# Retention and latent attention block: side work of VectorE moved behind the feature stage, first group's q, k, v copied by ScalarE with its gates ahead of its tiles

## The chip, the cores and the metric

The kernel runs on one core of one Trainium2 chip. The metric is the device time of one execution in microseconds (us). A core has five engines with their own instruction streams: PE (TensorE, matrix products), DVE (VectorE), ACT (ScalarE), POOL (GpSimd) and SP (SyncE, which here only issues DMAs). They wait for each other through semaphores. SBUF is the on-chip memory; PSUM is the memory that PE writes, in eight banks.

## The reference

One encoder block on x, 1024 positions by 1024 features in float32. A modulation that depends on c scales and shifts the normalised x; one combined projection feeds two groups. Group A is retention in 8 heads: rotated q and k, v, a decay per head, chunks of 128 positions in both directions, a normalisation per head, and a SiLU gate. Group B is latent attention in 8 heads. Both are joined by an output projection, and added to x through a modulated gate. The part that matters here, for one direction (shortened):

```python
mask = diff >= 0 if include_diag else diff > 0
decay_intra = jnp.where(mask[None], jnp.exp(lg * jnp.maximum(diff, 0.0)[None]), 0.0)
scores = jnp.einsum('bhnik,bhnjk->bhnij', qc, kc) * decay_intra[None, :, None]
intra = jnp.einsum('bhnij,bhnjv->bhniv', scores, vc)
kv_chunk = jnp.einsum('bhnjk,bhnjv->bhnkv', kc * k_decay[None, :, None, :, None], vc)
def step(state, kv):
    return state * chunk_decay + kv, state
cross = jnp.einsum('bhnik,bhnkv->bhniv', qc * q_decay[None, :, None, :, None], states)
```

## The kernel before, in words

Each float32 product is three matmuls of reduced operands: `mm3` (L64) adds hi by hi (L65), hi by lo (L66) and lo by hi (L67). The hi half of an operand is a cast by ScalarE, the lo half is the subtraction raw minus hi. For weights that is `split` (L75): the cast is L80 on ACT, the subtraction L81, on POOL unless `eng` says otherwise. A weight page of 128x1024 is loaded by `wpage` (L84) into `wr` (two buffers) and then split into `wh` and `wl` (seven buffers each).

*The opening.* For each of 8 tiles of 128 rows, `x_tile` (L148) squares x on ACT (L156) or, for the tiles in `XDVE`, on DVE (L152), raises the mean to the power -0.5 on POOL (L158), scales on DVE (L159), transposes on PE (L163, eight blocks of 128x128), and copies the two PSUM banks out, the first by ACT (L166), the second by DVE (L168). For each of 8 blocks k of 128 features, `modulation(k)` (L174) makes two numbers per feature with two 128x1024 products on DVE (L178) and two small steps (L181, L183), and `features(k, half)` (L186) applies them on ACT (L188), casts to hi on ACT (L189) and subtracts to lo on DVE (L190). `products(k, lo, hi)` (L199) then adds block k to q, k and v of four tiles of the first head group; all eight PSUM banks hold these sums (`acc0`, four of the tag acc, four of sm). That is 192 matmuls of 512 columns. The pages of the first group's weights are split on DVE (L196).

*Side work.* L235 to L260 compute the logarithms of the decays (`lg`, `kfac`), L267 `qfac` by an exponential on ACT, L270 and L271 the operands of the eight masks on DVE, L272 their exponentials on ACT, L274 a scale. L280 to L316 compute the rotary angles in `rtmp` on DVE (reduction in the steps of L291), and `Sr` and `Cr` by a sine on ACT (L313, L316). ACT loads another table when the function changes its set.

*The four head groups.* For each group g the loop over 8 tiles (L344) takes the projected tile (for g = 0 from `acc0`, else from 24 new matmuls), copies v out by ACT (L355), for four banks of group 0 also q and k (`xq`, L360), rotates q and k on DVE (L364, L366) and POOL (L370, L371), prepares kd (L374), transposes on PE (L379), copies qT and kz by ACT (L381, L384), multiplies by the decays (L386), makes scores (L390) and masks them (L392), makes the chunk's k-v product (L397), and folds it into the running state `ST` (L401 to L408). A backward recurrence on DVE ends it (L411). Then come the gate of two heads, 96 matmuls of 512 columns per head (`gate`, L418), whose SiLU by ACT is `sg` (L426), and two `outputs` (L429): products of scores and states (L437, L438), a copy by ACT (L440), statistics (L443), normalisation (L450). `finish` (L453), which transposes (L457), scales by the gate (L459) and stores, waits in a list `pending` until `turn_outputs` (L333) runs it behind a chosen product.

*What sets the order.* The program is written in the order above, but a scheduler moves the instructions of each engine by estimated times, within their dependencies and within the reach of buffers; each engine then runs its own list strictly in that order. `tc.issue_after(x)` says that an instruction is not put ahead of x. The constants at the end of the file (`XDVE`, `KACT`, `PEND` and others) choose these places. A PSUM bank or a buffer is free for its next use when the last reader has ended.

## Time and profile before

| quantity | value |
|---|---|
| median of 3 runs | 1044.26 us (1044.09 to 1044.92) |
| profiled execution, its own time | 1045.73 us |
| span of the profile, first to last instruction | 1043.7 us |
| PE busy | 1011.9 us, 97% of the span |
| DVE, ACT, POOL busy | 562.5, 431.0, 395.2 us |
| mean granted clock of PE | 0.987 |

Busy means that an instruction of the engine was under way. The granted clock is the share of its full clock that PE was given; a value of 1 is 2.4 GHz. An execution's own time is that of its span and what lies around it. In a timeline a row that ends in x16 is a run of 16 like instructions with the time of all; the number in brackets is the idle time before it and what ended it.

### The profile page before, as it was taken

How to read it: one execution, taken by the hardware profiler on the slowest of the kernel's cores; microseconds unless marked ns; L12 is line 12 of the kernel's file. 1: busy time of each engine (PE TensorE's matmuls, PEld its weight loads, DVE VectorE, ACT ScalarE, POOL GpSimd, SP SyncE). 2: the span in 40 equal slices, each digit the busy share in tenths (PEclk: the TensorE clock that was granted, in tenths of full speed). 3: DMA queues.
4: the chain of work that ended last, by engine and by line, in shares of the span. 5: the costliest groups of instructions: out<-in, count | busy, mean ns of one | idle time of the engine just before them, and what ended most of it. 6: DMA issues, size and time to landing. Idle time of an engine off the chain costs nothing.

```text
span 1043.7 us, 15236 instructions
## 1 busy us (share of the span) xinstructions
PE 1011.9 (97%) x5704; PEld 883.0 (85%) x5704; DVE 562.5 (54%) x1287; ACT 431.0 (41%) x873; POOL 395.2 (38%) x359
## 2 busy tenths in 40 slices
PE   5899999999999999999999999999999999989998
PEld 4677888888888888998888889889999999878887
DVE  7995447445444434046302116857777777883342
ACT  6654213312311321224322007577777776762100
POOL 3233315313321522224653213633456544864110
PEclk6999999999999999999999999999999999999999
DMA  9721103101211202323554520100000000004422
GB/s 372 264 66 56 41 1 112 50 1 62 66 36 41 66 27 86 110 93 130 185 175 159 191 94 11 41 1 2 21 21 21 2 21 22 21 21 129 164 101 71
DMA packets 30744, 82.27 MB, mean 79 GB/s; under 512 B 3536, under 2 KB 4560, under 8 KB 30672
## 3 DMA queue, kind: packets, MB, share of 16 engines
q1 hardware_dynamic: 25920, 72.92, 20.8%
q10 hardware_dynamic: 4752, 8.39, 2.2%
q8 instruction: 45, 0.74, 0.3%
q14 instruction: 27, 0.22, 0.1%
HBM read 64.52 MB, written 16.78 MB: 78 GB/s over the span
## 4 chain that ended last, share of the span: by engine, by line
PE 47%; DVE 4%; POOL 1%; ACT 1%; issue 1%; DMA 0%; ACTq 0%; POOLq 0%; DVEq 0%
PE pt L772 5%; PE sp L65 4%; PE sp L66 4%; PE sp L67 4%; PE acc L67 4%; PE acc L66 4%; PE acc L65 4%; PE po L66 3%; PE po L67 3%; PE po L65 3%; PE sm L66 1%; PE sm L65 1%; PE sm L67 1%; PE pt L685 1%; DVE q L659 1%; PE pt L66 1%
## 5 line engine op out<-in xcount | busy, mean ns | idle before, releaser
L81 POOL TENSOR_TENSOR wl<-wr,wh 128x1024 fp32r<-128x1024 f32 (+2 forms) x51 | 115.3, 2268 | 129.8 <-ACT wh L80 111.7
L65 PE MATMUL acc<-wh,hh 128*128 128x512 f32 (+2 forms) x352 | 130.4, 370 | 1.7 <-ACT hh L189 1.7
L66 PE MATMUL acc<-wl,hh 128*128 128x512 f32 (+2 forms) x352 | 130.3, 370 | 0.0
L67 PE MATMUL acc<-wh,hl 128*128 128x512 f32 (+2 forms) x352 | 126.4, 367 | 1.9 <-DVE hl L190 1.9
L758 POOL TENSOR_SCALAR pr<-pr,st 128x1024 f32<-128x1024 f32 x62 | 71.0, 1148 | 101.2 <-DVE st L757 70.0
L65 PE MATMUL acc<-hh,wh 128*128 128x512 f32 x256 | 101.9, 398 | 2.2 <-ACT v L355 2.2
L775 DVE TENSOR_TENSOR pl<-pt,ph 128x512 fp32r<-128x512 f32 x128 | 85.7, 684 | 32.0 <-ACT ph L774 32.0
L66 PE MATMUL acc<-hl,wh 128*128 128x512 f32 x256 | 101.5, 396 | 0.0
L67 PE MATMUL acc<-hh,wl 128*128 128x512 f32 x256 | 101.1, 395 | 0.0
L80 ACT CAST wh<-wr 128x1024 fp32r<-128x1024 f32 (+2 forms) x55 | 53.7, 982 | 106.4 <-PE sm L66 36.6
L774 ACT CAST ph<-pt 128x512 fp32r<-128x512 f32 x128 | 73.3, 590 | 27.1 <-PE pt L772 25.1
L753 DVE TENSOR_REDUCE st<-sp 128x1 f32<-128x1024 f32 x62 | 75.4, 1216 | 8.0 <-PE sp L67 7.9
L66 PE MATMUL po<-pl,vh 128*128 128x256 f32 x256 | 76.0, 297 | 2.3 <-DVE pl L775 2.3
L756 ACT ACTIVATE pr<-sp,st 128x1024 f32<-128x1024 f32 x62 | 69.5, 1122 | 20.7 <-DVE st L754 20.5
L370 POOL TENSOR_TENSOR rb<-t,t 128x128 f32<-128x128 f32 x32 | 16.0, 501 | 161.9 <-PE sm L379 61.2
L65 PEld LDWEIGHTS acc<-wh,hh 128*128 128x128 f32 x352 | 66.9, 190 | 10.6 <-ACT hh L189 2.3
L67 PEld LDWEIGHTS acc<-wh,hl 128*128 128x128 f32 x352 | 66.0, 188 | 10.6 <-DVE hl L190 2.7
L66 PEld LDWEIGHTS acc<-wl,hh 128*128 128x128 f32 x352 | 66.9, 190 | 8.5
L65 PE MATMUL po<-ph,vh 128*128 128x256 f32 x256 | 73.3, 286 | 0.0
L772 PE MATMUL pt<-ident,pr 128*128 128x128 f32 x496 | 69.8, 273 | 2.8 <-DVE st L757 1.2
L67 PE MATMUL po<-ph,vl 128*128 128x256 f32 x256 | 72.4, 283 | 0.0
L772 PEld LDWEIGHTS pt<-ident,pr 128*128 128x128 f32 x496 | 57.6, 140 | 7.3 <-issue 1.4
(361 smaller groups left out, 2449.0 us busy)
## 6 DMA issues: line engine op xcount, KB each, us to landing
x<-w_ada SPq DMA_DIRECT2D x16, 512.0 KB, 6.8
wr<-w_ret SPq DMA_DIRECT2D x16, 512.0 KB, 3.5
wr<-w_rg SPq DMA_DIRECT2D x8, 512.0 KB, 3.5
retD<-ro SPq DMA_DIRECT2D x16, 256.0 KB, 2.0
wr<-w_mg SPq DMA_DIRECT2D x8, 512.0 KB, 3.6
wa<-w_ada SPq DMA_DIRECT2D x8, 512.0 KB, 3.6
wr<-w_out SPq DMA_DIRECT2D x8, 512.0 KB, 4.0
wro<-retD SPq DMA_DIRECT2D x8, 512.0 KB, 3.9
```

The source lines that it names most:

```text
L65: T.matmul(out, lh, rh, start=first, stop=False, **kw)
L66: T.matmul(out, lh, rl, start=False, stop=False, **kw)
L67: return T.matmul(out, ll, rh, start=False, stop=last, **kw)
L80: A.copy(out=hi, in_=raw)
L81: eng.tensor_tensor(out=lo, in0=raw, in1=hi, op=ALU.subtract)
L370: G.tensor_tensor(out=rv[:, :, 0], in0=t1[:, :, 0], in1=t2[:, :, 1], op=ALU.subtract)
L753: V.tensor_reduce(out=st_[:, 0:1], in_=sp, op=ALU.max, axis=AX.X)
L756: A.activation(pr, sp, AF.Exp, bias=st_[:, 1:2], scale=sc_, accum_out=st_[:, 2:3])
L758: G.tensor_scalar(out=pr, in0=pr, scalar1=st_[:, 3:4], scalar2=0.0, op0=ALU.mult, op1=ALU.add)
L772: T.transpose(tp[:, ts_(q)], pr[:, ts_(half * 4 + q)], ident)
L774: A.copy(out=ph[half][:, :, c_], in_=tv)
L775: V.tensor_tensor(out=pl[half][:, :, c_], in0=tv, in1=ph[half][:, :, c_], op=ALU.subtract)
```

## The change

The square of tile 3 goes from DVE to ACT, and for tiles 0 to 3 ACT makes both copies out of PSUM. The two small steps of `modulation` go to ACT. The polynomial for the decays is issued behind a subtraction of feature block 1 (`KDEC`), masks and angles behind that of block 5 (`KACT`). In group 0, ACT copies v and q, k of all eight tiles out of PSUM into SBUF; the gate is computed ahead of the tiles, with its two weight pages split on DVE and not on POOL, issued behind the features of block 6 (`KWG`); the tiles follow the last product of the first head's gate. The weight pages of groups 0 and 1 are issued behind the last features, and both output halves of group 0 are turned in group 1, at tiles 1 and 2.

```diff
@@ -81,10 +81,10 @@
         eng.tensor_tensor(out=lo, in0=raw, in1=hi, op=ALU.subtract)
         return hi.rearrange(*shape[0], **shape[1]), lo.rearrange(*shape[0], **shape[1])
 
-    def wpage(src, n, k, pool=None, tag="wr", bufs=2):
+    def wpage(src, n, k, pool=None, tag="wr", bufs=2, eng=G):
         raw = (pool or p_ring).tile([P, n], F32, name="wr", tag=tag, bufs=bufs)
         SY.dma_start(out=raw, in_=src)
-        return split(raw, (("p (k n) -> p k n",), {"k": k}))
+        return split(raw, (("p (k n) -> p k n",), {"k": k}), eng=eng)
 
     ps1 = ExitStack()
     pp = ps1.enter_context(tc.tile_pool(name="ps1", bufs=1, space=PSUM, reuse_waits="tile"))
@@ -162,7 +162,7 @@
             for q in range(4):
                 T.transpose(ps[:, ts_(q)], x_[:, ts_(4 * z + q)], ident)
             dst, src = xn[:, 4 * z:4 * z + 4, ts_(t)], ps.rearrange("p (a b) -> p a b", a=4)
-            if z == 0:
+            if z == 0 or t < 4:
                 A.copy(out=dst, in_=src)
             else:
                 V.tensor_copy(out=dst, in_=src)
@@ -178,17 +178,16 @@
             V.scalar_tensor_tensor(out=wa, in0=wa, scalar=1.0, in1=sc, op0=ALU.mult, op1=ALU.mult,
                                    accum_out=mp[:, i:i + 1])
         b1 = p_st.tile([P, 2], F32, name="b1", tag="b1", bufs=3)
-        V.scalar_tensor_tensor(out=b1[:, 0:1], in0=mp[:, 0:1], scalar=nw[:, k:k + 1], in1=c1[:, k:k + 1],
-                               op0=ALU.mult, op1=ALU.add)
-        V.tensor_tensor(out=b1[:, 1:2], in0=mp[:, 1:2], in1=bada[:, k:k + 1], op=ALU.add)
+        A.activation(b1[:, 0:1], mp[:, 0:1], AF.Identity, bias=c1[:, k:k + 1], scale=nw[:, k:k + 1])
+        A.activation(b1[:, 1:2], mp[:, 1:2], AF.Identity, bias=bada[:, k:k + 1])
         b1s[k] = b1
 
     def features(k, half):
         sl = slice(half * 512, half * 512 + 512)
         A.activation(xn[:, k, sl], xn[:, k, sl], AF.Identity, bias=b1s[k][:, 1:2], scale=b1s[k][:, 0:1])
         i0 = A.copy(out=hh[k][:, sl], in_=xn[:, k, sl])
-        V.tensor_tensor(out=hl[k][:, sl], in0=xn[:, k, sl], in1=hh[k][:, sl], op=ALU.subtract)
-        return i0
+        i1 = V.tensor_tensor(out=hl[k][:, sl], in0=xn[:, k, sl], in1=hh[k][:, sl], op=ALU.subtract)
+        return i0, i1
 
     w0, acc0 = [], []
 
@@ -227,8 +226,16 @@
             if k or half:
                 i0 = features(k, half)
                 products(k, 4 * half, 4 * half + 4)
+            if k == KDEC:
+                v_first = i0[1]
+            if k == KWG:
+                f_wg = i0[0]
             if k == KACT:
-                x_last = i0
+                x_last, v_last = i0
+
+    f_last = i0[0]
+    late = ExitStack()
+    late.enter_context(tc.issue_after(v_first.ins))
 
 
     lg = ctile("lg", 16)
@@ -259,6 +266,8 @@
     A.activation(kfac[:, :, 1], lg[:, 8:16], AF.Exp, scale=rowc[:, 1:2])
     V.tensor_scalar(out=kfac, in0=kfac, scalar1=0.125, scalar2=None, op0=ALU.mult)
 
+    late.close()
+    late.enter_context(tc.issue_after(v_last.ins))
     qfac = p_rc.tile([P, H, P], F32, name="qfac", tag="qfac")
     mask = p_rc.tile([P, H, P], F32, name="mask", tag="mask")
     after = ExitStack()
@@ -316,6 +325,7 @@
     A.activation(Cr, nn, AF.Sin)
     after.__exit__(None, None, None)
 
+    late.close()
     st.close()
 
 
@@ -336,28 +346,62 @@
             pending.pop(0)()
 
     for g in range(4):
+        after = ExitStack()
+        if g < 2:
+            after.enter_context(tc.issue_after(f_last.ins))
         w = w0 if g == 0 else [wpage(I["w_ret"][g][j], 1024, 2) for j in range(4)]
-        vv = []
+        after.close()
+        vv, xqs = [], []
+
+        wg, sg = [], []
+
+        def gate_begin():
+            sg.append(p_ret.tile([P, 2, S], F32, name="sg", tag="sg"))
+            with tc.issue_after(f_wg.ins):
+                wg.extend(wpage(I["w_rg"][g][j], 1024, 4, eng=V if g == 0 else G) for j in range(2))
+
+        def gate(h):
+            for half in range(2):
+                ps = acc()
+                for k in range(KT):
+                    wh, wl = wg[k // 4]
+                    rh = hh[k][:, half * 512:half * 512 + 512]
+                    rl = hl[k][:, half * 512:half * 512 + 512]
+                    last = mm3(ps, wh[:, k % 4, ts_(h)], wl[:, k % 4, ts_(h)], rh, rl, k == 0, k == KT - 1)
+                A.activation(sg[0][:, h, half * 512:half * 512 + 512], ps, AF.Silu)
+            return last
+
+        if g == 0:
+            for t in range(NT):
+                vv.append(p_ret.tile([P, 2, P], F32, name="v", tag="v", bufs=9))
+                xqs.append(p_ret.tile([P, 2, P], F32, name="xq", tag="sT", bufs=8).rearrange("p a b -> p (a b)"))
+                A.copy(out=xqs[t], in_=acc0[t][:, 0:256])
+                A.copy(out=vv[t].rearrange("p h d -> p (h d)"), in_=acc0[t][:, 256:512])
+            gate_begin()
+            last = gate(0)
+            gate(1)
+            after = ExitStack()
+            after.enter_context(tc.issue_after(last.ins))
         ST = p_ret.tile([P, NT, 2, P], F32, name="ST", tag="ST")
         sT = [None] * NT
         qdT = [None] * NT
         for t in range(NT):
-            if g == 0 and t < NB0:
+            if g == 0:
                 ps = acc0[t]
+                v_ = vv[t]
             else:
                 ps = acc()
                 for k in range(KT):
                     wh, wl = w[k // 2]
                     last = mm3(ps, hh[k][:, ts_(t)], hl[k][:, ts_(t)], wh[:, k % 2], wl[:, k % 2], k == 0, k == KT - 1)
-                if pending and t == PEND:
+                if pending and t in (PEND, PEND + 1):
                     turn_outputs(last)
-            v_ = p_ret.tile([P, 2, P], F32, name="v", tag="v", bufs=9)
-            A.copy(out=v_.rearrange("p h d -> p (h d)"), in_=ps[:, 256:512])
-            vv.append(v_)
+                v_ = p_ret.tile([P, 2, P], F32, name="v", tag="v", bufs=9)
+                A.copy(out=v_.rearrange("p h d -> p (h d)"), in_=ps[:, 256:512])
+                vv.append(v_)
             xq = ps[:, 0:256]
-            if g == 0 and NACC <= t < NB0:
-                xq = p_ret.tile([P, 256], F32, name="xq", tag="o", bufs=5)
-                A.copy(out=xq, in_=ps[:, 0:256])
+            if g == 0:
+                xq = xqs[t]
             xq = xq.rearrange("p (a d) -> p a d", d=32)
             t1 = p_ret.tile([P, 4, 2, 32], F32, name="t1", tag="t1", bufs=2)
             t2 = p_ret.tile([P, 4, 2, 32], F32, name="t2", tag="t2", bufs=2)
@@ -406,25 +450,13 @@
                                                op0=ALU.mult, op1=ALU.add)
             if t > 0:
                 A.copy(out=ST[64:128, t - 1], in_=kvv[64:128])
+        if g == 0:
+            after.close()
         for t in range(NT - 2, 0, -1):
             for h in range(2):
                 V.scalar_tensor_tensor(out=ST[64:128, t - 1, h], in0=ST[64:128, t, h],
                                        scalar=gch[64:128, 2 * g + h:2 * g + h + 1], in1=ST[64:128, t - 1, h],
                                        op0=ALU.mult, op1=ALU.add)
-
-
-        wg = [wpage(I["w_rg"][g][j], 1024, 4) for j in range(2)]
-        sg = p_ret.tile([P, 2, S], F32, name="sg", tag="sg")
-        def gate(h):
-            for half in range(2):
-                ps = acc()
-                for k in range(KT):
-                    wh, wl = wg[k // 4]
-                    rh = hh[k][:, half * 512:half * 512 + 512]
-                    rl = hl[k][:, half * 512:half * 512 + 512]
-                    last = mm3(ps, wh[:, k % 4, ts_(h)], wl[:, k % 4, ts_(h)], rh, rl, k == 0, k == KT - 1)
-                A.activation(sg[:, h, half * 512:half * 512 + 512], ps, AF.Silu)
-            return last
 
         def outputs(half):
             mv = p_ret.tile([P, 4, 2, 2], F32, name="mv", tag="mv", bufs=2)
@@ -457,10 +489,15 @@
                         T.transpose(tp[:, ts_(q)], ob[q][:, h], ident)
                     ro = p_ret.tile([P, 512], F32, name="ro", tag="ro", bufs=2)
                     V.scalar_tensor_tensor(out=ro, in0=tp, scalar=gnw[:, 2 * g + h:2 * g + h + 1],
-                                           in1=sg[:, h, half * 512:half * 512 + 512], op0=ALU.mult, op1=ALU.mult)
+                                           in1=sg[0][:, h, half * 512:half * 512 + 512], op0=ALU.mult, op1=ALU.mult)
                     SY.dma_start(out=retD[2 * g + h, :, half * 512:half * 512 + 512], in_=ro)
             pending.append(finish)
 
+        if g == 0:
+            outputs(0)
+            outputs(1)
+            continue
+        gate_begin()
         gate(0)
         outputs(0)
         last = gate(1)
@@ -921,7 +958,7 @@
 PREP_0 = (2, 4, 5, 6, 6)
 NB0, NACC, XW = 8, 4, 8
 WLX = (6, 7)
-XDVE, KACT = (3, 6), 1
+XDVE, KDEC, KACT, KWG = (6,), 1, 5, 6
 MG0 = 2
 PEND = 1
 EARLY = (2, 6)
```

Three places show how the lists of the engines change. The rows have line, operation, output from input, shape. The first is ScalarE from the last features to the first copies out of PSUM; `Sr`, `Cr` are the rotary tables, `mask` and `mt` the decay masks and their operands. Before:

```order
L272 ACTIVATE mask<-mt 128x128 x2
L189 CAST hh_91<-xn 128x512 x2
L272 ACTIVATE mask<-mt 128x128 x2
L80 CAST wh<-wr 128x1024
L313 ACT_TABLE_LOAD
L313 ACTIVATE Sr<-rtmp 128x256
L316 ACTIVATE Cr<-rtmp 128x256
L80 CAST wh<-wr 128x1024
L355 COPY v<-acc 128x256 x4
L355 COPY v<-sm 128x256
L360 COPY xq<-sm 128x256
```

and now:

```order
L263 ACTIVATE gch<-lgs 128x8
L276 ACTIVATE qfac<-small,lgs 128x128 x8
L325 ACT_TABLE_LOAD
L325 ACTIVATE Cr<-rtmp 128x256
L281 ACT_TABLE_LOAD
L281 ACTIVATE mask<-mt 128x128 x2
L80 CAST wh<-wr 128x1024
L281 ACTIVATE mask<-mt 128x128 x2
L80 CAST wh<-wr 128x1024
L281 ACTIVATE mask<-mt 128x128 x4
L378 COPY xq<-acc 128x256
L379 COPY v<-acc 128x256
```

The factors and masks, which stood between the features, stand behind them, next to the tables, and the copies stand behind all of it.

The second is VectorE around the last feature subtractions (`hl_97` to `hl_99` are the lo halves of blocks 5 to 7). Before:

```order
L190 TENSOR_TENSOR hl_97<-xn,hh_89 128x512
L271 SCALAR_TENSOR_TENSOR mt<-small,lg,m_693 128x128
L190 TENSOR_TENSOR hl_97<-xn,hh_89 128x512
L295 TENSOR_TENSOR rtmp<-rtmp 128x256
L291 SCALAR_TENSOR_TENSOR rtmp<-rtmp 128x256
L270 TENSOR_SCALAR m_699<-small,lg 128x128
L190 TENSOR_TENSOR hl_98<-xn,hh_90 128x512
L291 SCALAR_TENSOR_TENSOR rtmp<-rtmp 128x256
L271 SCALAR_TENSOR_TENSOR mt<-small,lg,m_699 128x128
L190 TENSOR_TENSOR hl_98<-xn,hh_90 128x512
L291 SCALAR_TENSOR_TENSOR rtmp<-rtmp 128x256
L270 TENSOR_SCALAR m_705<-small,lg 128x128
```

and now:

```order
L189 TENSOR_TENSOR hl_97<-xn,hh_89 128x512 x2
L289 CAST posf<-pos 128x8
L189 TENSOR_TENSOR hl_98<-xn,hh_90 128x512 x2
L249 TENSOR_TENSOR lt_627<-lt_626 128x16
L292 TENSOR_TENSOR rtmp<-small,posf 128x256
L189 TENSOR_TENSOR hl_99<-xn,hh_91 128x512
L252 TENSOR_TENSOR lt_628<-lt_628,lt_627 128x16
L296 TENSOR_SCALAR rtmp<-rtmp 128x256
L311 COPY rtmp<-rtmp 128x256
L81 TENSOR_TENSOR wl<-wr,wh 128x1024
L253 TENSOR_SCALAR lt_628<-lt_628 128x16
L297 TENSOR_SCALAR rtmp<-rtmp 128x256
L81 TENSOR_TENSOR wl<-wr,wh 128x1024
```

The mask operands and angle steps that stood between the subtractions have moved behind them, and two page subtractions (L81) have come in ahead of the last.

The third is TensorE at tiles 6 and 7 of group 0 (`qT`, `kz` are operands of the scores, `rb` rotated q and k, `ST` the states, `hh`, `hl`, `wh`, `wl` the operands of a 512-column product). Before:

```order
L65 MATMUL acc<-wh,hh_90 128x512
L66 MATMUL acc<-wl,hh_90 128x512
L67 MATMUL acc<-wh,hl_98 128x512
L390 MATMUL sm<-qT,kz_753 128x128 x2
L397 MATMUL sm<-v,kd 128x128 x2
L437 MATMUL sm<-v,sT 128x128 x2
L65 MATMUL acc<-wh,hh_91 128x512
L66 MATMUL acc<-wl,hh_91 128x512
L67 MATMUL acc<-wh,hl_99 128x512
```

and now:

```order
L434 MATMUL sm<-qT,kz_753 128x128 x2
L441 MATMUL sm<-v,kd 128x128 x2
L423 MATMUL sm<-ident,rb_750 128x128 x3
L65 MATMUL acc<-wh,hh_91 128x512
L66 MATMUL acc<-wl,hh_91 128x512
L67 MATMUL acc<-wh,hl_99 128x512
L434 MATMUL sm<-qT,kz_752 128x128
L441 MATMUL sm<-v,kd 128x128 x2
L434 MATMUL sm<-qT,kz_752 128x128
L423 MATMUL sm<-ident,rb_751 128x128 x3
L434 MATMUL sm<-qT,kz_753 128x128 x2
L441 MATMUL sm<-v,kd 128x128 x2
L469 MATMUL sm<-v,sT 128x128 x4
```

The 512-column products that stood between the steps of the last tiles and the outputs now stand ahead of them and behind them.

## Rows read from the trace of the kernel before

**Rows 1.** The waits of PE: line, waited for, total us, times, longest.

```profile
PE sm L65 <- ACT hh L189: 2.6, 1, 2.6
...
PE acc L65 <- ACT v L355: 2.2, 1, 2.2
...
PE acc L67 <- DVE hl L190: 1.9, 1, 1.9
...
PE sm L67 <- DVE hl L190: 0.9, 1, 0.9
...
PE sm L457 <- DVE o L450: 0.6, 1, 0.6
```

**Rows 2.** Busy us (instructions) by stretch, all engines; PEclk; DMA share; GB/s.

```profile
20.00:30.00 10.00, 8.79 (x39) 7.39 (x40) 10.00 (x22) 4.87 (x8) 3.76 (x2) 0.64 1.03 409
...
80.00:90.00 10.00, 7.91 (x30) 6.44 (x31) 7.21 (x16) 7.50 (x19) 7.46 (x8) 0.83 0.29 93
```

**Rows 3.** Timeline of PE: start, duration, line, operation, idle before.

```profile
33.36 0.50 PE L65 MATMUL sm<-wh,hh 128*128 128x512 f32 x1 [2.60 <-ACT hh L189]
...
79.50 0.39 PE L67 MATMUL sm<-wh,hl 128*128 128x512 f32 x1
82.09 0.77 PE L65 MATMUL acc<-hh,wh 128*128 128x512 f32 x1 [2.20 <-ACT v L355]
82.65 0.63 PE L66 MATMUL acc<-hl,wh 128*128 128x512 f32 x1
```

**Rows 4.** Groups of VectorE by form, 10 to 73 us: count, busy us, mean ns.

```profile
L190 DVE TENSOR_TENSOR hl<-xn,hh 128x512 fp32r<-128x512 f32 x16 | 12.9, 818 | 0.0
...
L270 DVE TENSOR_SCALAR m<-small,lg 128x128 f32<-128x128 f32 x8 | 4.4, 550 | 0.0
L181 DVE SCALAR_TENSOR_TENSOR b<-mp,small,c 128x1 f32<-128x1 f32 x8 | 3.8, 470 | 0.0
...
L271 DVE SCALAR_TENSOR_TENSOR mt<-small,lg,m 128x128 f32<-128x128 f32 x8 | 2.7, 341 | 0.0
L168 DVE COPY xn<-acc 128x512 f32<-128x512 f32 x4 | 2.7, 682 | 0.0
```

**Rows 5.** Timeline of VectorE, late features.

```profile
49.21 3.41 DVE L178 SCALAR_TENSOR_TENSOR x<-x,sc 128x1024 f32<-128x1024 f32 x1
...
72.29 0.68 DVE L190 TENSOR_TENSOR hl<-xn,hh 128x512 fp32r<-128x512 f32 x1
...
77.36 0.88 DVE L291 SCALAR_TENSOR_TENSOR rtmp<-rtmp 128x256 f32<-128x256 f32 x2
```

**Rows 6.** Timeline of POOL at 45 us.

```profile
45.60 5.93 POOL L81 TENSOR_TENSOR wl<-wr,wh 128x1024 fp32r<-128x1024 f32 x2 [18.62 <-ACT wh L80]
```

**Rows 7.** Timeline of ScalarE, 36 to 88 us.

```profile
37.61 1.86 ACT L267 ACTIVATE qfac<-small,lgs 128x128 f32<-128x128 f32 x6
...
78.60 0.42 ACT L313 ACTIVATE Sr<-rtmp 128x256 f32<-128x256 f32 x1 [3.65 <-DVE rtmp L310]
...
79.84 1.04 ACT L80 CAST wh<-wr 128x1024 fp32r<-128x1024 f32 x1
80.79 1.19 ACT L355 COPY v<-acc 128x256 f32<-128x256 f32 x4
...
87.44 0.54 ACT L384 COPY kz<-sm 64x128 f32<-64x128 f32 x2
```

**Rows 8.** Timeline of ScalarE at the start: a table load and the next instruction.

```profile
3.77 1.28 ACT L238 ACT_TABLE_LOAD   x1
5.06 0.22 ACT L238 ACTIVATE lt<-lt 128x16 f32<-128x16 f32 x1
```

**Rows 9.** Timeline of VectorE, groups 0 and 1.

```profile
137.16 3.31 DVE L411 SCALAR_TENSOR_TENSOR ST<-ST,gch 64x128 f32<-64x128 f32 x12 [0.42 <-ACT ST L408]
...
150.96 2.15 DVE L450 TENSOR_SCALAR o<-o,mv,rst 128x128 f32<-128x128 f32 x8 [2.06 <-POOL rst L62]
157.47 1.41 DVE L459 SCALAR_TENSOR_TENSOR ro<-sm,small,sg 128x512 f32<-128x512 f32 x2 [4.36 <-PE sm L457]
```

## The prediction

> **What bounds the kernel now.** I read the waits of PE first, because PE is busy for 97% of the span and a change can win only where PE stands still. [rows 1] have all there is of that between the opening's transposes and the last groups: 2.6 us at the first steady product (it waits for a cast of ScalarE), 1.9 and 0.9 us at products that wait for the low half from VectorE, 2.2 us at the first gate product (it waits for a PSUM bank, which a copy of v frees), and 0.6 us at the outputs of the retention groups. So the most that the opening can give back is these 7.6 us and whatever lets the first product start earlier.
>
> Second, the busy time by stretch of 10 us [rows 2]: VectorE reads 10.00 of 10 (the six stretches from 10 to 70 us read 9.96 to 10.00), so in the features VectorE sets the pace and PE follows. The timeline of PE gives three marks [rows 3]: the steady products start at 33.36, the last one at 79.50, the gate at 82.09. With a spacing of 0.227 us the products end near 79.73. Behind the 2.2 us of standing, the first gate products are 0.43 us apart instead of 0.227, and the mean granted clock of 80 to 90 us is 0.83 [rows 2]: PE runs at 1.2 GHz and not 2.4 for about 3 us after an idle stretch.
>
> Third, what VectorE does there, by kind [rows 4], and single instructions [rows 5]. A modulation product of 1.22 us takes 3.41 us at 49.21, while POOL subtracts two weight pages [rows 6]. The same 2.1 to 2.2 us is in the totals of L270 (4.4 us for eight of 0.28), of L181 (3.8 us for eight of 0.21) and of L190 (12.9 us for sixteen of 0.68). So one page that POOL subtracts can hold VectorE for about 2.2 us; it happened four times in the features, 9 us in all.
>
> **The change, part by part.**
>
> *VectorE's features end earlier.* They take 61.9 us now, from 11.0 to 72.9, where the last L190 ends [rows 5]. What leaves that stretch, by [rows 4]: mask operands 4.4 + 2.7; the small bias L181 3.8, and about 1 for L183; the PSUM copies of the first four tiles 2.7; one square, about 1.2; the angle steps, seven L291 at no more than 0.44 [rows 5], 2.9, with their companions and the polynomial about 2.6; the locks in L178 and L190, 2.2 each. That is 25.7 us busy. Consecutive instructions overlap by some 0.07 us, 3 us over 45 of them, so 22.7 us of time. Two gate pages that VectorE now subtracts itself add 2.3, small steps 1.3. So 43 us of work remain. It can no longer run without a gap, since it will wait for casts and loads; I take 4 us of that (0 to 8). The features end on VectorE at 58 (54 to 62), 15 us earlier.
>
> *PE's features.* The first steady product waits for a chain in which about 3 us of VectorE's work no longer stands (0 to 6): 30.3. With the 2.8 us of waits on L190 gone, the last product ends at 79.73 - 3.06 - 2.96 = 73.7 (the two waits with a few tenths beside them). The 0.2% that a measurement of this kernel can tell from no change is 2.1 us; up to here the change would be worth 6 us.
>
> *The gate can't start there.* Now the side work is late. In the new order of ScalarE, the copies that free the PSUM banks stand behind Sr, kfac, eight qfac, Cr, eight masks and two page casts, and Sr stands behind nearly all angle steps on VectorE. Before, ScalarE did qfac and masks inside the features, and only Sr, Cr and one cast stood ahead of the copies, with Sr waiting 3.65 us for VectorE [rows 7]. From the end of VectorE's features: ten L291 at 0.34 to 0.44, and 25 smaller steps at about 0.1 to 0.3, 6.3 us to Sr's input; two page subtractions of POOL fall there at 2.2 us each, a third perhaps: 10.9 to 13.3. Then on ScalarE [rows 7, 8]: Sr 0.42, table load 1.28, kfac and chunk factors 0.5, qfac 8 x 0.31 = 2.5, load 1.28, Cr 0.42, load 1.28, masks 8 x 0.25 = 2.0, two casts 2.1, two copies 0.7: 12.5. Together 23.4 to 25.8. Two more pages can lock the mask operands, 0 to 4.4 us; I take half, because it hangs on when the pages land. The sum is 26.4 behind 58: the gate starts at 84.4 and not 82.09, **+2.3 us**. Its bounds: not before PE's last product plus a cast, four masks and two copies, 76.4 (-5.7), and not behind 62 + 30 with every lock, less what the loads hide, 89 (+7). I don't go to the ends, because both halves of this chain are priced by rows. PE stands for some 11 us there; the slow 3 us behind it existed before.
>
> The Trainium skill, SBUF — State Buffer, section Who interferes with whom, says that VectorE and GpSimd hold a shared port as a lock for a whole instruction, and that an instruction with two SBUF inputs or a tensor-scalar one in a fast mode is exposed to it. Every mask operand is of these kinds; by that rule alone both pages would lock, and the gate would start 2.2 us later than I take, the total then being 1058.0. [rows 5] agree as to the price, and no run here yet shows whether those pages meet the masks.
>
> The Trainium skill, ScalarE: Activation LUTs, section What ACT_TABLE_LOAD costs, adds a drain of about 1.4 us to every load; with three loads on this path that would be some 4 us more by an estimate from that page. [rows 8] disagree: after a load of 1.28 us the next instruction starts 1.29 us after the load's start.
>
> *New stretches with nothing to fill them.* Before, group 0's tiles ran between gate products and group 1's q, k, v products, and PE lost nothing there beyond 0.6 us. Now the gate's 192 products come first or early and three places hold only tile and output steps. (1) Tiles 6 and 7 with outputs 0: copies of qT and kz 0.9 [rows 7], a copy of the state 0.5, eleven steps of the backward recurrence at 3.31 / 12 = 0.276 [rows 9], 3.0, two rope products 0.75 ahead of the next bank, less 0.8 of PE's own work, 4.35; a smaller wait ahead of it 0.5. (2) The transposes of the first outputs, with a tile: two L459 steps 1.4 [rows 9], copies 0.9, ropes on VectorE 0.75 and on POOL 0.85: 3.9. (3) The second half's transposes behind four normalising steps at 2.15 / 8 = 0.27 [rows 9]: 1.0. Sum 9.75, less the 0.6 that goes: **+9.2 us** (2 if the steps run ahead of PE; 12 at most if PE falls to 1.2 GHz after each).
>
> *At nothing:* the copies of q, k, v out of all banks (16 at 0.27 to 0.30 us apiece on ScalarE [rows 7]): behind the first two PE has 43 us of gate products to cover them. The later loads of group 1's pages: they are due 40 us later. If the gate were short of them it would show as a wait for a cast of L80. POOL loses two subtractions.
>
> *Sum.* 2.3 + 9.2 = +11.5. The profiled execution took 1045.73 us (span 1043.7, 2.0 around it), so 1057.2 on its terms; it was 1.47 above the median of the runs, 1044.26, so 1055.8 against that.
>
> **The rivals.**
> - *Cover holds.* The features end early on VectorE (54 or so), POOL's pages land between its steps and not on them, and the gate starts at 76.4 to 77; tile steps run ahead of PE and lose only 2 us. For it: VectorE has 15 us of new room. Against: ScalarE's 12.5 us remain. Gain 5.7 - 2 to 3, time **1041**, chance 0.16. It decides at a gate start below 78.
> - *Nothing won.* Gate at 78.5 (-3.6), the three stretches 3.6: **1044.3**, chance 0.08.
> - *Only the gate is late.* +2.3 and the stretches lose under 1: **1046.9**, chance 0.17. For it speaks that PE lost 0.6 in such places; against it, that then q, k, v products stood between.
> - *All of it.* Locks on the masks, gate at 89 (+7), the stretches 9.2, and 3 us more at 1.2 GHz: **1063**, chance 0.12.
> - *ScalarE takes over the features*, since it gets the copies, the square and sixteen small steps: then PE's features end at 79 or so, but the gate is set by the side work in any case, and the sum stays. It is part of the forecast.
>
> **How the numbers follow.** Forecast 0.47 at 1055.8, its own range 1051 to 1060. Faster 0.16 is the first rival; same 0.08 the second; slower the rest, 0.76. Range: from 1042.5, which leaves out most of the first rival, to 1063, which leaves out the worst of the last.
>
> **What would show it.** VectorE's last L189 near 58; PE's last feature product near 73.7; a wait of PE of 9 to 12 us at the first gate product, released by a copy on ScalarE; POOL's page subtractions over VectorE's angle steps with 2 us extra each; waits of PE at the outputs and transposes of group 0 of 4 and 4 us where there were none. The forecast is wrong if the gate starts before 78, or if PE's waits from there to group 2 add up to less than 4 us.

## The result, and the profile after

The changed kernel takes **1060.17 us** (median of 5 runs, 1058.96 to 1061.23), the kernel before 1044.92 in the same comparison (5 runs). The ratio is 1.0144, 95% interval 1.0133 to 1.0155: 15.2 us slower. The forecast was 1055.8 with a range of 1042.5 to 1063, so sign and range held, and the loss was some 4 us larger (15.2 for 11.5). The profiled execution took 1060.17 us with a span of 1058.0; against [rows 1], [rows 2] and [rows 3] this is what changed. The page has the engines' busy time, and the group that carries the loss:

```profile
PE 1012.6 (96%) x5704; PEld 883.7 (84%) x5704; DVE 552.9 (52%) x1267; ACT 442.3 (42%) x902; POOL 387.8 (37%) x357
...
L65 PE MATMUL acc<-hh,wh 128*128 128x512 f32 x256 | 102.2, 399 | 14.7 <-ACT v L379 13.8
```

PE does the same work (1012.6 us busy, 1011.9 before) and stands still for longer. The waits of PE (line, waited for, total us, times, longest), where [rows 1] had 2.6 + 2.2 + 1.9 + 0.9 + 0.6:

```profile
PE acc L65 <- ACT v L379: 13.8, 1, 13.8
...
PE sm L65 <- ACT hh L188: 3.1, 1, 3.1
...
PE sm L434 <- ACT kz L428: 2.0, 3, 0.7
...
PE sm L470 <- DVE ST L457: 1.0, 1, 1.0
PE acc L65 <- DVE t L410: 1.0, 1, 1.0
PE sm L489 <- DVE ro L491: 0.8, 1, 0.8
...
PE sm L423 <- ACT o L472: 0.3, 1, 0.3
```

The waits on L190 are gone. One wait of 13.8 us stands before the first gate product. Five groups of waits that were not there, 5.1 us together, stand at scores, outputs and transposes of groups 0 and 1. The timeline of PE (start, duration, and in brackets the idle time before it) has the three marks of [rows 3], and the end of the second of those stretches:

```profile
73.96 0.39 PE L67 MATMUL sm<-wh,hl 128*128 128x512 f32 x1
88.12 0.80 PE L65 MATMUL acc<-hh,wh 128*128 128x512 f32 x1 [13.77 <-ACT v L379]
88.71 0.63 PE L66 MATMUL acc<-hl,wh 128*128 128x512 f32 x1
...
93.83 0.53 PE L66 MATMUL acc<-hl,wh 128*128 128x512 f32 x1
...
190.31 0.50 PE L65 MATMUL acc<-hh,wh 128*128 128x512 f32 x1 [0.96 <-DVE t L410]
```

The features end on PE 5.5 us earlier than before (73.96 for 79.50), the gate starts 6.03 us later (88.12 for 82.09), and the products at 1.2 GHz, 0.43 us apart, last until 94 instead of 85.5 (the granted clock is 0.50 from 80 to 90 us and 0.79 from 90 to 100). Fourteen steps take 6.08 us there instead of 14 x 0.227, which is 2.9 lost; before it was eight in 3.40, 1.6 lost. To see what lies behind the gate's start I count: up to the 193rd hi-by-hi product of 512 columns (the rows of L65 in order) PE has the same features, gate and group 1 behind it, in every kernel here. It starts at 212.67, before at 198.82. So from the gate's start to there it took 124.55 us instead of 116.73. 6.03 + 7.82 = 13.85 of the 14.4 us between the two profiled executions.

What ScalarE does ahead of that first gate product, and VectorE and POOL beside it, again from the timeline of the changed kernel, one engine after the other:

```profile
68.37 1.05 ACT L80 CAST wh<-wr 128x1024 fp32r<-128x1024 f32 x1 [4.89 <-DMA wr<-w_ret]
69.44 1.28 ACT L322 ACT_TABLE_LOAD   x1
70.74 0.42 ACT L322 ACTIVATE Sr<-rtmp 128x256 f32<-128x256 f32 x1
...
75.41 1.28 ACT L325 ACT_TABLE_LOAD   x1
76.71 0.42 ACT L325 ACTIVATE Cr<-rtmp 128x256 f32<-128x256 f32 x1
...
84.78 0.31 ACT L281 ACTIVATE mask<-mt 128x128 f32<-128x128 f32 x1 [3.55 <-DVE mt L280]
...
87.69 0.38 ACT L379 COPY v<-acc 128x256 f32<-128x256 f32 x1
...
57.74 0.68 DVE L189 TENSOR_TENSOR hl<-xn,hh 128x512 fp32r<-128x512 f32 x1
...
62.51 2.37 DVE L253 TENSOR_SCALAR lt<-lt 128x16 f32<-128x16 f32 x1
...
65.13 2.37 DVE L252 TENSOR_TENSOR lt<-lt,lt 128x16 f32<-128x16 f32 x1
...
68.98 0.29 DVE L319 TENSOR_SCALAR rtmp<-rtmp 128x256 f32<-128x256 f32 x1
...
69.66 2.37 DVE L260 COPY lgs<-lg 64x8 f32<-64x8 f32 x1
...
78.78 0.35 DVE L280 SCALAR_TENSOR_TENSOR mt<-small,lg,m 128x128 f32<-128x128 f32 x1 [4.76 <-ACT mask L281]
...
79.94 2.44 DVE L279 TENSOR_SCALAR m<-small,lg 128x128 f32<-128x128 f32 x1
82.48 2.26 DVE L280 SCALAR_TENSOR_TENSOR mt<-small,lg,m 128x128 f32<-128x128 f32 x1
...
62.35 5.12 POOL L81 TENSOR_TENSOR wl<-wr,wh 128x1024 fp32r<-128x1024 f32 x2 [36.68 <-ACT wh L80]
69.50 2.49 POOL L81 TENSOR_TENSOR wl<-wr,wh 128x1024 fp32r<-128x1024 f32 x1 [2.03 <-ACT wh L80]
79.95 4.64 POOL L81 TENSOR_TENSOR wl<-wr,wh 128x1024 fp32r<-128x1024 f32 x2 [7.96 <-DVE mt L280]
```

VectorE ends its features at 58.4 (57.74 and a pitch of 0.6). Then the five page subtractions of POOL each hold one of its instructions: a 128x16 step takes 2.37 us, a mask operand 2.44 and 2.26. Sr's input is ready at 69.3 (L319). Its table load stands behind a page cast at 68.37 that waited for its DMA, so Sr starts 1.5 us after its input. Four table loads lie on this path, those ahead of Sr, kfac, Cr and the masks. The masks wait for VectorE, VectorE waits 4.76 us for a mask to give back one of the two buffers, and the copies come last.

### The profile page after: what moved, and what is told of

Same layout as the page of the kernel before. It is cut to its first block, busy times and chain, and to the rows that moved or that the text cites. A ratio compares the mean times of both kernels' runs of the same rounds, so it can differ in the third digit from the quotient of the medians.

```text
span 1058.0 us, 15250 instructions
## 1 busy us (share of the span) xinstructions
PE 1012.6 (96%) x5704; PEld 883.7 (84%) x5704; DVE 552.9 (52%) x1267; ACT 442.3 (42%) x902; POOL 387.8 (37%) x357
## 4 chain that ended last, share of the span: by engine, by line
PE 45%; DVE 4%; ACT 1%; DMA 1%; issue 1%; POOL 1%; ACTq 0%; DVEq 0%; POOLq 0%
PE pt L809 5%; PE sp L65 4%; PE sp L67 4%; PE sp L66 4%; PE acc L67 4%; PE acc L65 4%; PE acc L66 4%; PE po L66 3%; PE po L67 3%; PE po L65 3%; PE sm L67 1%; PE sm L65 1%; PE sm L66 1%; DMA wa<-w_ada 1%; DVE q L696 1%; PE pt L722 1%
## 5 line engine op out<-in xcount | busy, mean ns | idle before, releaser
L81 POOL TENSOR_TENSOR wl<-wr,wh 128x1024 fp32r<-128x1024 f32 (+2 forms) x49 | 109.2, 2238 | 163.9 <-ACT wh L80 151.1
L65 PE MATMUL acc<-wh,hh 128*128 128x512 f32 (+2 forms) x352 | 130.7, 371 | 0.1
L65 PE MATMUL acc<-hh,wh 128*128 128x512 f32 x256 | 102.2, 399 | 14.7 <-ACT v L379 13.8
L65 PEld LDWEIGHTS acc<-wh,hh 128*128 128x128 f32 x352 | 67.0, 190 | 9.0 <-DVE t L410 0.3
L65 PE MATMUL po<-ph,vh 128*128 128x256 f32 x256 | 73.5, 287 | 0.0
L65 PEld LDWEIGHTS acc<-hh,wh 128*128 128x128 f32 x256 | 48.8, 190 | 25.0 <-ACT v L379 14.2
```

Of the source, the lines that this page charges most:

```text
L65: T.matmul(out, lh, rh, start=first, stop=False, **kw)
L81: eng.tensor_tensor(out=lo, in0=raw, in1=hi, op=ALU.subtract)
```

## The experiments

Twelve kernels ran beside the kernel before. The table has their medians, the ratio to before with its interval, the start of the first gate product, and the time from there to the 193rd product (before: 82.09 and 116.73).

| kernel | us | ratio | gate | to the 193rd |
|---|---|---|---|---|
| changed kernel | 1060.17 | 1.0144 (1.0133 to 1.0155) | 88.12 | 124.55 |
| pages late | 1050.35 | 1.0049 (1.0032 to 1.0066) | 79.08 | 126.60 |
| masks in place | 1053.80 | 1.0090 (1.0071 to 1.0110) | 83.37 | 123.97 |
| copies first | 1043.14 | 0.9985 (0.9975 to 0.9996) | 74.45 | 124.15 |
| second half only | 1045.02 | 0.9999 (0.9990 to 1.0008) | 76.92 | 121.63 |
| gate split | 1062.42 | 1.0162 (1.0144 to 1.0179) | 87.24 | 129.39 |
| copies first, gate split | 1046.04 | 1.0013 (1.0001 to 1.0024) | 73.99 | 124.96 |
| second half, gate split | 1047.32 | 1.0019 (1.0010 to 1.0028) | 76.69 | 124.51 |
| old order | 1052.83 | 1.0070 (1.0054 to 1.0087) | 88.10 | 117.24 |
| second half, old order | 1041.82 | 0.9970 (0.9961 to 0.9980) | 76.43 | 117.52 |
| side work early, old order | 1040.68 | 0.9956 (0.9943 to 0.9969) | 76.88 | 116.69 |
| pages late, old order | 1041.57 | 0.9968 (0.9956 to 0.9980) | 79.15 | 116.48 |
| gate pages alone | 1040.76 | 0.9957 (0.9943 to 0.9971) | 78.95 | 115.71 |

The last two columns are of the profiled execution, which is not always near the median: that of copies first was the longest of ten (1045.83), that of second half, old order the shortest of twelve (1039.22), that of old order the shortest of four (1050.55).

My theory: two independent losses, the gate late because the side work queues ahead of the copies, and stretches of small steps without products to fill them. The rivals: only one of them is real, or the first makes the second.

### The late gate: three ways to undo it

**Pages late.** Group 1's five pages are issued behind the last copy.

```diff
-            after.enter_context(tc.issue_after(f_last.ins))
+            after.enter_context(tc.issue_after((c_last if g else f_last).ins))
...
-            with tc.issue_after(f_wg.ins):
+            with tc.issue_after((c_last if g == 1 else f_wg).ins):
...
-                A.copy(out=vv[t].rearrange("p h d -> p (h d)"), in_=acc0[t][:, 256:512])
+                c_last = A.copy(out=vv[t].rearrange("p h d -> p (h d)"), in_=acc0[t][:, 256:512])
```

> The changed kernel, with the five weight pages of group 1 issued behind the last copy out of PSUM. Theory (the gate waits for side work that queues behind group 1's page casts on ScalarE and is held by POOL's subtractions on VectorE): without the two locks at 62.5 and 65.1 us Sr's input is ready 4.4 us earlier, at 64.7; loads, factors, qfac and Cr take 7.8 from there, the masks 3.1, a copy pair 0.5, so the gate starts at 76.5 and not 88.1; about 1 us less at 1.2 GHz; time 1047 to 1049. Rival A (only ScalarE's list counts, the pages don't): gate within 2 us of 88, time 1058 to 1061. Rival B (the pages come too late for group 1): a new wait of PE for a cast or a subtraction of a page at 120 us, and the gain is given back.

Measured 1050.35, over 1 us above the expected range. The gate came 9.0 us earlier, 2.6 later than I had worked out. The timeline of ScalarE shows where:

```profile
65.87 0.42 ACT L322 ACTIVATE Sr<-rtmp 128x256 f32<-128x256 f32 x1 [7.78 <-DVE rtmp L319]
...
73.57 0.51 ACT L281 ACTIVATE mask<-mt 128x128 f32<-128x128 f32 x2
...
75.85 0.31 ACT L281 ACTIVATE mask<-mt 128x128 f32<-128x128 f32 x1 [0.47 <-DVE mt L280]
...
78.19 0.31 ACT L281 ACTIVATE mask<-mt 128x128 f32<-128x128 f32 x1 [0.47 <-DVE mt L280]
```

Nothing of POOL is near, and still each mask follows the one before by 0.78 us, with 0.47 of waiting for its operand: with two buffers the operand's instructions and the exponential alternate. Rival A fell, and rival B too: PE waits for no page. The time to the 193rd product grew by 2.0, because PE's clock now fell in the second stretch (0.70 from 180 to 190 us, 1.00 in the changed kernel).

**Masks in place.** The operand is written where its mask will stand.

```diff
-        mt = p_st.tile([P, P], F32, name="mt", tag="mt", bufs=2)
+        mt = mask[:, h]
```

> The changed kernel, with the operand of each mask written into the mask's own place instead of two alternating buffers, so that VectorE need not wait for ScalarE between masks. Theory: VectorE ends all mask operands at 78, before POOL's two pages at 80; ScalarE's casts and masks then run without the 3.55 + 3 x 0.5 us of waits; gate at 82.6 to 83.5, time 1054.5 to 1055.5. Rival (the locks at the masks are not what holds the gate, the page casts are): gate at 86 or later, time over 1058.

Measured 1053.80, a little below the range, with the gate at 83.37, inside it: 4.75 us of the late start were the masks' alternation with POOL's pages falling into it.

**Copies first.** On ScalarE, qfac, masks, Sr and Cr are issued behind the sixteen copies (the code of the side work is moved behind them, masks in place; the moved lines are left out here).

```diff
-    after.enter_context(tc.issue_after(x_last.ins))
...
+        after.enter_context(tc.issue_after(c_last.ins))
...
-                A.copy(out=vv[t].rearrange("p h d -> p (h d)"), in_=acc0[t][:, 256:512])
+                c_last = A.copy(out=vv[t].rearrange("p h d -> p (h d)"), in_=acc0[t][:, 256:512])
+            side(c_last)
```

> The changed kernel, with qfac, masks, Sr and Cr issued on ScalarE behind the sixteen copies out of PSUM (masks in place for space). Theory: the copies start when PE ends the features at 74.4, the gate at 74.9 instead of 88.1, without an idle stretch ahead of it and so without the thirteen products at 0.43 us (2.6 us): time 1044 to 1045.5, the three stretches of tile and output steps still being there at 7 to 8 us. Rival A (the side work, later still, now holds the tiles): a wait of PE at the first tile's transposes near 97 us and 1047 to 1055. Rival B (something other than the copies frees the gate): gate near 88, no change.

Measured 1043.14, 0.9 us below the range. The gate starts at 74.45, 0.7 us behind the start of the last hi-by-hi feature product, so nothing but ScalarE's list held it, and rival B fell. No wait of PE stands at the tiles' transposes behind it, so rival A fell too. In the profiled execution the slow products did not go away, however. They moved to the second stretch, as its timeline of PE shows:

```profile
173.68 0.80 PE L65 MATMUL acc<-hh,wh 128*128 128x512 f32 x1 [0.50 <-DVE t L414]
174.28 0.63 PE L66 MATMUL acc<-hl,wh 128*128 128x512 f32 x1
```

The busy time by stretch of the same kernel (engines as in [rows 2], then granted clock, DMA share, GB/s):

```profile
170.00:180.00 10.00, 8.60 (x30) 6.63 (x29) 6.91 (x29) 1.99 (x7) 3.69 (x5) 0.66 0.49 153
```

The granted clock of 170 to 180 us is 0.66, and products are 0.43 us apart there. The time to the 193rd product stayed at 124.15: the second loss is there without the first. That it is nearly the same number is chance, since the spell at 1.2 GHz left the gate and came up in the stretch; the second half alone, next, allows a cleaner comparison.

### The second half of the change alone

The opening is put back (`XDVE` (3, 6), VectorE's copies and small steps, no `late`), the order of group 0 stays.

```diff
-            if z == 0 or t < 4:
+            if z == 0:
...
-    late.enter_context(tc.issue_after(v_first.ins))
...
-    late.enter_context(tc.issue_after(v_last.ins))
...
-XDVE, KDEC, KACT, KWG = (6,), 1, 5, 6
+XDVE, KDEC, KACT, KWG = (3, 6), 1, 1, 6
```

> The second half of the change alone: the opening as before (side work between the features, squares, copies and small steps on the engines they had), the gates of group 0 ahead of its tiles, all banks copied by ScalarE, outputs late. Theory (the three stretches with nothing to fill them belong to the new order of group 0 and cost 7 to 8 us whatever the opening does; the late gate belongs to the opening): gate at 80 to 83, waits of PE between 120 and 200 us as in the changed kernel, time 1049 to 1053. Rival (the stretches come from the late side work): no waits there, time 1043 to 1046.

Measured 1045.02, no change, and below what I expected. The stretches are there, in the same five groups of waits, 5.1 us again, so the rival fell although the time is in its range. From the gate to the 193rd product it takes 121.63, 4.9 more than before, although no product ran at 1.2 GHz at the gate, which cost 1.6 before. Without what the products at 1.2 GHz cost (their spacing above 0.227 us), that way takes 121.5 to 121.7 us in all five kernels so far (changed, pages late, masks in place, copies first, second half only) and some 115.2 before: the new order costs 6.3 to 6.5 us there, whatever the opening does. But the gate is at 76.92, 5.2 earlier than before, which I had not seen coming. On ScalarE the first copies stand right behind Sr and one cast (timeline of ScalarE, then a row of VectorE):

```profile
74.66 0.42 ACT L320 ACTIVATE Sr<-rtmp 128x256 f32<-128x256 f32 x1 [3.76 <-DVE rtmp L317]
...
76.19 0.38 ACT L377 COPY v<-acc 128x256 f32<-128x256 f32 x1
...
76.32 2.47 DVE L408 TENSOR_TENSOR t<-xq,Sr 128x256 f32<-128x256 f32 x1 [0.91 <-ACT xq L376]
```

In this kernel the gate's pages are VectorE's own, and its features end on PE 2.8 us earlier (last hi-by-hi product at 76.24, before 79.05). The last row shows a price of copying q and k to SBUF: a rope product (the rotation of q and k by Sr or Cr) of 0.42 us takes 2.47 beside a page that POOL subtracts. Read from PSUM it was not held, as the kernel before shows in its first tiles (timeline of VectorE, then POOL):

```profile
81.53 0.41 DVE L366 TENSOR_TENSOR t<-acc,Sr 128x256 f32<-128x256 f32 x1
...
80.96 2.37 POOL L81 TENSOR_TENSOR wl<-wr,wh 128x1024 fp32r<-128x1024 f32 x1 [4.58 <-ACT wh L80]
```

The Trainium skill, SBUF — State Buffer, section Who interferes with whom, has that distinction (two SBUF inputs are exposed), and the trace agrees.

### Splitting the gate

The second head's gate stands behind outputs 0 again, alone, with the copies first, and with the old opening.

```diff
             last = gate(0)
-            gate(1)
...
-                if pending and t in (PEND, PEND + 1):
+                if pending and t == PEND:
...
             outputs(0)
+            last = gate(1)
+            turn_outputs(last)
             outputs(1)
```

> The changed kernel, with only the first head's gate ahead of group 0's tiles; the second head's gate stands behind outputs 0, and the first half is turned behind it, as before the change. Theory (the stretches cost what they do because the 192 gate products are used up before the last tiles and the outputs): gate still at 88; the second and third stretch (the transposes of the outputs, with waits of 0.84, 0.28, 0.62, 0.96 and 0.67 us in the changed kernel) get products between them and vanish, the first (tiles 6, 7 and outputs 0) stays, at 2 to 3 us; time 1055 to 1057. Rival (the stretches are set by the serial steps of VectorE and ScalarE and not by the order): within 1.5 us of the changed kernel.

> The copies ahead of the side work on ScalarE, and the split gate, together. Theory: the two losses are independent, so the gate starts at 75 and the 4 to 5 us of the second and third stretch go: 1043.1 less 4.4, 1038 to 1039.5. Rival (with the gate earlier, the side work reaches the tiles late): a wait of PE at the first tile's transposes, and 1041 or more.

> The opening as before, copies of all banks and the first head's gate ahead of the tiles, the second head's behind outputs 0. Theory: gate at 77 as in the run with both gates ahead, the second and third stretch gone: 1045.0 less 3 to 4.5, 1040.5 to 1042, and the changed opening is worth only the 2.4 us by which its features end earlier (1038 to 1039.5 for the other run of this call). Rival (the opening is worth its full 5.3 us): 1043 or more here with 1038 there.

All three missed: 1062.42, 1046.04 and 1047.32, each 2 to 3 us slower than its counterpart instead of 4 faster. None of the rivals fits whole either. The second and third stretch were not filled, they moved; the timeline of the first of the three, by engine:

```profile
179.20 0.49 PE L433 MATMUL sm<-qT,kz 128*128 128x128 f32 x2 [2.92 <-ACT kz L427]
...
184.64 0.79 PE L65 MATMUL acc<-hh,wh 128*128 128x512 f32 x1 [4.28 <-DVE t L409]
...
176.88 1.04 ACT L80 CAST wh<-wr 128x1024 fp32r<-128x1024 f32 x1 [5.25 <-DMA wr<-w_ret]
...
181.42 2.50 DVE L417 TENSOR_TENSOR kd<-rb,kfac 128x256 f32<-128x256 f32 x1
...
181.31 2.33 POOL L81 TENSOR_TENSOR wl<-wr,wh 128x1024 fp32r<-128x1024 f32 x1
```

ScalarE stood 5.25 us for the load of a page of group 2 and then had copies to catch up; kd, 0.4 us elsewhere, took 2.50 under a page subtraction, with the rope products that free PE's bank behind it, and PE waited 2.92 and 4.28 us. All three runs have this kd of 2.50 us and the 4.3 us behind it, followed by 8 to 14 products at 1.2 GHz. A hold of kd alone does not make such a wait. The changed kernel has one too (timeline of VectorE), but there the rope products that free PE's bank follow some 6 us later (189.84), and PE waits 0.96 us for them:

```profile
183.16 2.06 DVE L418 TENSOR_TENSOR kd<-rb,kfac 128x256 f32<-128x256 f32 x1
```

So my reason for the stretches (products used up too early) is incomplete: what the small steps cost depends as well on which of them a page falls on, and on what stands right behind that one.

### The order of before

**Old order.** The whole change but for the order of group 0: tiles first, then gates and outputs.

```diff
-            last = gate(0)
-            gate(1)
-            after = ExitStack()
-            after.enter_context(tc.issue_after(last.ins))
...
-                if pending and t in (PEND, PEND + 1):
+                if pending and t == PEND:
...
-        if g == 0:
-            outputs(0)
-            outputs(1)
-            continue
-        gate_begin()
+        if g:
+            gate_begin()
```

> The changed opening, and ScalarE's copies of all banks, but group 0 in the order of before: tiles, then gates, outputs, turned as before. Theory (the late gate belongs to the opening's side work, whatever comes first behind it): the first product behind the features starts at 87 to 89, the three stretches are gone but for about 1 us: 1052 to 1054.5. Rival (the gates ahead of the tiles cause the late start too): first product before 84 and 1050 or less.

Measured 1052.83, as expected. PE waits for nothing between its gate's start and 480 us, so the stretches are gone with the order alone, and the start is late as in the changed kernel (timeline of PE):

```profile
88.10 0.80 PE L65 MATMUL acc<-hh,wh 128*128 128x512 f32 x1 [13.95 <-ACT v L379]
```

**Three versions that keep a part.** Second half with the old order (the opening of before, copies of all banks, gate pages on VectorE); the same with the copies, square and small steps of the opening on ScalarE, but the side work early (`late` left out, `KACT` 1); the late pages with the old order.

> The opening as before, ScalarE's copies of all banks and the gate pages of group 0 split on VectorE, but group 0 in the order of before (tiles, then gates and outputs). Theory (two independent losses, and one gain that both hide): the gate starts at 77 (5.2 less than before the change), without the idle stretch and so without the eight products at 0.43 us (1.6 less), and the three stretches are filled: 1045.2 - 6.8 = 1038.5, 1037.5 to 1040. Rival (the earlier gate is paid back later, because the tiles' side work or group 1's pages are then late): 1042 or more, with a wait of PE between 77 and 200 us.

> As the other run, with the copies of the first tiles, the square and the small steps on ScalarE too, the side work staying between the features. Theory (relieving VectorE in the opening is a gain, and only the delay of the side work a loss): the features end on PE between 73.5 and 76, the gate starts within 1 us of that, 1036.5 to 1039. Rival (VectorE needs the delay of the side work for that, ScalarE becomes the pace): the features end at 76 or later, and no gain over the other run.

> The changed opening with group 1's pages issued behind the copies, and the order of before in group 0. Theory (the losses add): gate at 79 as in the run with late pages, the stretches gone as in the run with the old order: 1045.2 - 3.0 + 0.5 = 1042.7, 1041.5 to 1044. Rival (the pages, issued late, fall on the tiles' VectorE steps): waits of PE of over 2 us between 120 and 200 us.

Measured 1041.82, 1040.68 and 1041.57: all faster than before. The third is as expected. In the other two the gate's start was right (76.43, 76.88) and the time over 1.5 us above the expected range. Why the first's median is above it, its trace can't tell, since the profiled execution took 1039.22 us, inside the range. What the trace does show is 2.4 us given back between 160 and 183 us, at the normalising steps of the second outputs, on which two pages of POOL fall (timeline of VectorE and PE):

```profile
164.90 6.57 DVE L474 TENSOR_SCALAR o<-o,mv,rst 128x128 f32<-128x128 f32 x8 [1.22 <-POOL rst L62]
...
170.19 1.67 PE L481 MATMUL sm<-ident,o 128*128 128x128 f32 x5 [1.29 <-DVE o L474]
```

Before the change the same steps are held as long, also by two pages:

```profile
167.69 6.28 DVE L450 TENSOR_SCALAR o<-o,mv,rst 128x128 f32<-128x128 f32 x8 [0.69 <-POOL rst L62]
...
172.57 0.50 PE L457 MATMUL sm<-ident,o 128*128 128x128 f32 x2 [0.60 <-DVE o L450]
...
173.17 0.48 PE L65 MATMUL acc<-hh,wh 128*128 128x512 f32 x1
```

So the pages are not the difference. Before, gate products stand between the transposes of these outputs and PE waits 0.60 us; here none are left there, and it waits 1.29.

In the second, the features end on PE as without ScalarE's help (last hi-by-hi product at 76.09, in the first at 75.75), as its rival had it: the copies, the square and the small steps bought nothing on PE when the side work stays early. Its time is 1.1 us below the first's, less than the spread of the runs of either.

**Gate pages alone.** The kernel before with one thing of the change:

```diff
-    def wpage(src, n, k, pool=None, tag="wr", bufs=2):
+    def wpage(src, n, k, pool=None, tag="wr", bufs=2, eng=G):
...
-        return split(raw, (("p (k n) -> p k n",), {"k": k}))
+        return split(raw, (("p (k n) -> p k n",), {"k": k}), eng=eng)
...
-        wg = [wpage(I["w_rg"][g][j], 1024, 4) for j in range(2)]
+        wg = [wpage(I["w_rg"][g][j], 1024, 4, eng=V if g == 0 else G) for j in range(2)]
```

> The kernel before, with one thing of the change: the two gate pages of group 0 are split by VectorE (1.14 us each) and not by POOL, whose subtraction held VectorE for 2.2 us a page where it met it. Theory (the lock is what the features paid, 4.4 us for these two pages): PE's features end at 76 to 77 instead of 79.7, the gate starts at 78.5 to 80 instead of 82.1, time 1041.5 to 1043. Rival (the lock falls on side work that nobody waits for, or the next pages take its place): features end within 1 us of before, time 1044 to 1046.

Measured 1040.76, 0.7 us below the expected range, 4.5 us faster than before and as fast as any version here. PE's waits for the low halves (L190), 2.8 us before, are 0.3, the last hi-by-hi feature product starts 2.9 us earlier, and the gate at 78.95, with no product at 0.43 us behind it (1.6 us less). Its timeline of VectorE and POOL:

```profile
52.33 1.22 DVE L81 TENSOR_TENSOR wl<-wr,wh 128x1024 fp32r<-128x1024 f32 x1
...
57.56 6.90 DVE L190 TENSOR_TENSOR hl<-xn,hh 128x512 fp32r<-128x512 f32 x4
...
58.31 5.60 POOL L81 TENSOR_TENSOR wl<-wr,wh 128x1024 fp32r<-128x1024 f32 x2 [30.86 <-DVE hl L190]
```

Two subtractions of 1.22 us on VectorE replace two holds of about 2.2. Other pages of POOL still hold the features (four L190 in 6.90 us), at a place where PE is not yet waiting.

## Why the prediction was right, and where it was off

**VectorE's and PE's features: right.** 58 forecast, 58.4 measured; 73.7 forecast for the end of the last product, 74.2 measured (73.96 and a pitch of 0.227). The 3.06 us earlier start came out as 2.6 (30.78), of which some 2.1 were left once the products of both kernels ran at 2.4 GHz; the waits on L190 went.

**The gate can't start there: right in mechanism, short by 3.7 us.** 84.4 forecast, 88.12 measured, near the upper end of 89 that I gave. Three runs show the mechanism: with the copies first the gate follows the features at once, with the pages away it comes 9.0 us earlier, with the masks' buffers changed 4.75. Sr's input was ready at 69.3, where 69 to 71 was forecast. From there the sum had 14.7 us (12.5 and half of 4.4), and it took 18.9 (the input came some 0.4 earlier than the sum had it). Three terms were mis-sized. The sum counts three table loads; the load ahead of Sr was not among them, and the cast that waited for its page held it back: 1.5 us. "Masks 8 x 0.25 = 2.0": with two buffers they follow each other by 0.78, some 4.8 for eight (pages late shows it without any lock). "I take half" of the two locks: both hit (2.44 and 2.26), because the alternation kept VectorE at the masks until the pages landed. Masks, locks and the two casts together took 9.0 us, where the sum had 6.3; the casts ran while ScalarE would have waited. The sentence on the rule of the Trainium skill, that both pages would lock, was the better one; the trace agrees with it. The drain of the Trainium skill, ScalarE: Activation LUTs, section What ACT_TABLE_LOAD costs, did not show: Cr starts 1.30 us after the start of the load before it (75.41, 76.71).

**New stretches: right in sign and place, sized 9.2, measured 6.5.** Of the 7.8 us that are lost behind the gate's start, 1.3 is the longer spell at 1.2 GHz, which I had at nothing ("the slow 3 us behind it existed before"). The rest is the stretches: 4.5 are the new waits less the 0.6 that went, and 2.0 are small steps that follow each other slowly without a wait that the view counts. The waits that I named, of 4 and 4 us, were 1.7 at the outputs and 2.7 at the transposes (0.67 + 0.98 and 0.84 + 0.28 + 0.62 + 0.96 in the timeline of PE); the backward recurrence, put at 3.0, left PE 1.0 to wait. Old order shows that the order of group 0 makes the stretches. That products used up early are all of the cause, as I argued, is not shown: the split gate should then have helped, and did not. In the changed kernel the trace bounds the other part: of VectorE's steps in the three stretches only kd meets a page for long, and that costs at most 1.7 us (2.06 for 0.40) of the 6.5. A kernel without pages there was not tried.

**The sum and the rivals.** The gate was 3.7 us short and the spell at 1.2 GHz was left out, 1.3; the stretches were 2.7 too large. That the sum is nearer than its parts is luck. 1060.17 lies just outside the forecast's own 1051 to 1060 and nearer to the rival "all of it" (1063), whose locks on the masks and gate at 89 all but came true; its stretches and its 3 us more at 1.2 GHz did not. "Only the gate is late", "cover holds" and "nothing won" fell, and ScalarE did not take over the features. What no part of the working had: that the pages which the change gives to VectorE are a gain of some 4 us by themselves. I counted the four locks out of the features' work, but let the side work eat what that freed. In steps from run to run: from before to side work early with the old order, 4.1 less (gate pages alone gives 4.5 less); with the side work late, 12.1 more (1052.83); with the gates ahead of the tiles, 7.3 more (1060.17). Each step leads to the kernel of the next, so that they add up to the loss is no test; what they show is how large each part is.

## What to carry to other kernels

Moving work off the engine that sets the pace helps only if what it is moved behind does not free anything that the bound engine needs next: here sixteen copies stood behind side work that had been hidden. Before moving an engine's work, look for the single instructions that take several times their usual length; giving two 128x1024 subtractions to the engine that they were holding won 4.5 us with one argument. And when order fills the bound engine's gaps, list what the small steps between are exposed to, page loads and another engine's long instructions included.

## What the runs showed of the hardware that was not expected

A POOL subtraction of 128x1024 can hold even a VectorE instruction of 128x16 or 64x8 until it ends (2.37 us for 0.17). An idle stretch of 1.9 us on PE (gate pages alone) was followed by no product at 1.2 GHz, one of 2.2 (before) by some eight, one of 4.4 (pages late with the old order, gate at 79.15) by seven, one of 13.8 by some thirteen. And in the second stretch, where PE did 128-column steps with waits of under 1 us each, the clock fell in some kernels (0.66 from 170 to 180 with the copies first) and not in the changed one (1.00 from 180 to 190), though the steps are the same ones and the waits nearly so. Why is not shown.
